# Both MLP up-projections computed with the tokens, not the weights, as the stationary operand

## The chip, the cores and the metric

The kernel runs on one core of one Trainium2 chip. The metric is the device time of one execution in microseconds (us), the median of several runs. TensorE (PE in the rows; PEld is its weight load) multiplies, VectorE (DVE) and ScalarE (ACT) work elementwise, GpSimd (POOL) sets a few constants and issues a few transfers, and SyncE (SP) issues the large ones.

## The reference

Two transformer-like blocks over 256 tokens of width 2048: a gated linear attention block with an MLP, then a block of three branches (windowed attention, a linear recurrence, a short convolution) with an MLP. All inputs are float32. The change concerns the two MLPs alone, which have this form, with 2048 inputs, 8192 hidden columns and 2048 outputs:

```python
def _sq_relu_mlp(h, w_up, w_down):
    a = jax.nn.relu(h @ w_up)
    return (a * a) @ w_down
...
x = x + jnp.square(jax.nn.relu(h @ w_mlp_up[l])) @ w_mlp_down[l]
```

The scale of the normalisation in front of an MLP is applied after its down-projection, since relu and square let a positive factor through.

## The kernel before

**Jobs, chunks and halves.** Every large product is a job: 512 columns of a weight matrix (`KB`) against 128-row pieces of the contraction, called k-tiles; 16 of them in an up-projection job, 32 in a down-projection job. The weights come in chunks of four k-tiles (1 MB, `raw`, three buffers). A half is two k-tiles, and an up-projection job has 8 halves, a down-projection job 16. The 32 up-projection jobs (two MLPs, two groups `hf` of 4096 hidden columns, eight jobs `jn` in each group) have 256 halves. A group's eight up-projection jobs are followed by its four down-projection jobs, so the hidden values of one group live at a time.

**Three products for one.** Each float32 operand is split into a high part that TensorE takes exactly (fp32r) and the remainder. For the weights `split_half` does this for each half: ACT copies 128x1024 elements into `wh` (L186), DVE subtracts to get `wl` (L187). `wh` and `wl` have four buffers each, and `run` splits up to three halves (`LOOK`) ahead of the half that TensorE multiplies. The activations are split in the same way into tiles of [128, 2, 2, 256]: two k-tiles, high and low part, 256 tokens. `x` high times `w` high, `x` high times `w` low and `x` low times `w` high are summed in PSUM.

**Two forms of a job.** In a plain job (`products`) 128 tokens of an activation tile are the stationary operand and 512 weight columns stream past. For each k-tile and each of two groups `t` of 128 tokens there are three matmuls of 512 columns, so a half has 12 matmuls and 6144 columns; the result, [tokens, 512 columns], lies in two PSUM banks. In a swapped job (`swapped`) 128 columns of the weights are stationary and the activations stream: for each k-tile and each of four column groups `n` there is one matmul of 512 columns (`wh` against the high and the low part together, `long`) and one of 256 (`wl` against the high part, `short`). A half has 16 matmuls and 6144 columns, and the result, [columns, tokens], lies in four banks. PSUM has six banks for `acc`. Before the change the up-projections are swapped jobs, since the down-projection wants the hidden values with the hidden columns on the partitions, and a swapped job delivers them so.

**What follows a job.** A job's `ev` is a generator. `tick`, called once after each half, advances one of the waiting generators by a step (two where five or more wait), behind that half's splits in each engine's queue. After an up-projection job `ev` (L637) adds the two halves of each bank with `g_sum` (ACT copies, L330; DVE adds, L331), squares the positive part (L643), and splits into `h` tiles (L647, L651). A down-projection asks for the `h` tiles of up-projection job `jn` at its half 2 x `jn`.

**Turning.** `g_turn` exists before the change, for four stages in which token-order values are split for a later product (for instance after the jobs on `w_out`, L1018, called out2 below, whose jobs are plain and have 8 halves). DVE transposes 32x32 blocks of two 128x512 tiles into `blk` (L294, one buffer). Then 16 copies of 32 partitions move the blocks to their places in `turned`, in four steps of two DVE copies (L305) and two ACT copies (L303). Then come the splits, one pair of k-tiles in a step.

Of the kernel before, what the change touches and what calls it, by code (L numbers as in the profile page):

```python
# [8 lines left out]
F32 = mybir.dt.float32  # L9
F32R = mybir.dt.float32r  # L10
AF = mybir.ActivationFunctionType
ALU = mybir.AluOpType
# [26 lines left out]
def two_blocks(tc, A, out):  # L39
    nc = tc.nc  # L40
    es = ExitStack()
    with es:
# [10 lines left out]
        V, ACT, PE, POOL = nc.vector, nc.scalar, nc.tensor, nc.gpsimd  # L53

        def slot(shape, dt=F32, name="s"):
            return slp.tile(shape, dt, name=name, tag="s")

        def t2(name="t2", shape=(128, 512)):
            return t2p.tile(list(shape), F32, name=name, tag="t2")

        def t1(name="t1"):
            return t1p.tile([128, 256], F32, name=name, tag="t1")
# [7 lines left out]
        def flat(ap):  # L70
            return ap.rearrange("p a b -> p (a b)")
# [36 lines left out]
        def drain(key):  # L108
            rec = gens[key]
            while not rec[2]:  # L110
                if isinstance(rec[1], tuple):
                    drain(rec[1])
                advance(rec)
# [5 lines left out]
        cols = cp.tile([128, 164], F32, name="cols")  # L119
# [143 lines left out]
        def act_tile(name):  # L263
            return slot([128, 2, 2, 256], F32R, name)
# [19 lines left out]
        def split_any(d, src, pr, cols, mul):  # L284
            if cols is None:
                split_pair(d, src, mul)
            else:
                split_cols(d, src, cols[2 * pr:2 * pr + 2])

        def g_turn(full, name, b, cols, mul):  # L290

            blk = t2p.tile([128, 2, 4, 4, 32], F32, name="blk", tag="blk", bufs=1)
            for t in range(2):
                V.transpose(blk[:, t].rearrange("p f q c -> p (f q c)"), full(t))  # L294
            turned = slot([128, 4, 256], F32, "turned")
            to = turned.rearrange("p f (t q c) -> p f t q c", t=2, q=4)
            fr = blk.rearrange("p t f q c -> p f t q c")
            for a in range(4):
                yield 0
                for z in range(4):  # L300
                    o, i = to[32 * z:32 * z + 32, :, :, a, :], fr[32 * a:32 * a + 32, :, :, z, :]
                    if z % 2:
                        ACT.activation(o, i, AF.Copy)  # L303
                    else:
                        V.tensor_copy(o, i)  # L305
            for pr in range(2):
                yield 0
                d = T[name, 2 * b + pr] = act_tile("a")
                split_any(d, turned[:, 2 * pr:2 * pr + 2, :], pr, cols, mul)

        def g_split(full, name, b, cols=None, mul=None):
            if b < 3:
                yield from g_turn(full, name, b, cols, mul)
                return

            def src(t, i):
                return full(t)[:, i * 128:(i + 1) * 128]
            tps = [pair_transpose(src, 0)]
            yield 0
            tps.append(pair_transpose(src, 1))  # L320
            for pr in range(2):
                d = T[name, 2 * b + pr] = act_tile("a")
                split_any(d, tps[pr], pr, cols, mul)
                if pr == 0:
                    yield 0

        def g_sum(acc, dst):
            for n in range(4):
                r = t1("right")
                ACT.activation(r, acc[n][:, 256:512], AF.Copy)  # L330
                V.tensor_tensor(dst[:, n, :], acc[n][:, 0:256], r, op=ALU.add)  # L331
# [31 lines left out]
        def xblk(t, b):  # L363
            return xres[:, t, b * KB:(b + 1) * KB]
# [11 lines left out]
        T = {}  # L376
# [32 lines left out]
        def acts(name):  # L409
            return lambda k: T[name, k // 2][:, k % 2]  # L410
# [205 lines left out]
        def job(w, c0, nk, act, ev, key, need=None, pre=None, swap=False):  # L616
            jobs.append(Job(w[:, c0:c0 + KB], list(range(nk)), act, ev, key, need, pre, swap))
# [16 lines left out]
        def mlp(tag, w_up, w_down, xname, xkeys, rskey, rsq, ev_last):  # L634
            for hf in range(2):
                for jn in range(8):
                    def ev(acc, hf=hf, jn=jn):  # L637
                        y = slot([128, 4, 256], F32, "up")
                        g_sum(acc, y)
                        yield 0  # L640
                        for p in range(2):
                            v = flat(y[:, 2 * p:2 * p + 2, :])
                            V.scalar_tensor_tensor(v, v, 0.0, v, op0=ALU.max, op1=ALU.mult)  # L643
                        yield 0
                        for p in range(2):
                            d = T[tag, hf, 2 * jn + p] = act_tile("h")
                            ACT.activation(d[:, :, 0, :], y[:, 2 * p:2 * p + 2, :], AF.Copy)  # L647
                        yield 0
                        for p in range(2):
                            d = T[tag, hf, 2 * jn + p]  # L650
                            V.tensor_tensor(d[:, :, 1, :], y[:, 2 * p:2 * p + 2, :], d[:, :, 0, :].bitcast(F32), op=ALU.subtract)  # L651
                    job(w_up, hf * 4096 + jn * KB, 16, acts(xname), ev, (tag + "up", hf, jn),
                        (lambda k: ((xkeys, k // 4),)) if hf == 0 and jn == 0 else None, swap=True)
                for n in range(4):
                    def lhs(k, hf=hf):
                        return T[tag, hf, k // 2][:, k % 2]
                    if hf == 0:
                        def ev(acc, n=n):
                            drain(rskey)
                            for t in range(2):  # L660
                                V.scalar_tensor_tensor(xblk(t, n), acc[t], rsq[:, t:t + 1], xblk(t, n), op0=ALU.mult, op1=ALU.add)
                            yield 0
                    else:
                        ev = ev_last(n)
                    job(w_down[hf * 4096:(hf + 1) * 4096, :], n * KB, 32, lhs, ev, (tag + "dn", hf, n),
                        (lambda k, hf=hf: ((tag + "up", hf, k // 4),)) if n == 0 else None,
                        pre=pre_dn.get((tag, hf, n)))
# [30 lines left out]
        def ev_last1(n):  # L698
# [10 lines left out]
            return f  # L709

        mlp("m1", A["mlp_w_up"][0], A["mlp_w_down"][0], "x2", "out1", "rs2", T["rs2q"], ev_last1)


# [322 lines left out]
        def ev_last2(n):  # L1036
# [28 lines left out]
            return final if n == 3 else f  # L1065

        mlp("m2", A["w_mlp_up_2"][0], A["w_mlp_down_2"][0], "x5", "out2", "rs5", T["rs5q"], ev_last2)


# [81 lines left out]
```

## Time and profile before

| | us |
|---|---|
| median of 3 runs (2684.74 to 2685.83) | 2685.81 |
| profiled execution, device time | 2687.48 |
| its span, first to last instruction | 2685.7 |
| TensorE busy in the span | 2664.9 |
| VectorE busy | 1656.4 |
| ScalarE busy | 1315.5 |
| mean transfer rate | 191 GB/s |

The span of the profiled execution leaves out 1.78 us of its device time. A matmul's record lasts longer than the distance to the next one, since matmuls are pipelined: the pace is read from how many start in a stretch, not from a record's duration. Mean granted TensorE clock over the span is 0.998 of the full 2.4 GHz.

### The profile page before, as it was taken

The numbers are of one execution on the slowest core, as the hardware profiler recorded it, in microseconds if no ns is written. First come the engines' busy times: TensorE is split into PE (matmuls) and PEld (weight loads), VectorE is DVE, ScalarE is ACT, GpSimd is POOL, SyncE is SP. The second block draws the span as 40 slices with busy tenths as digits, with TensorE's granted clock in tenths as the row PEclk, the third lists the DMA queues.
The fourth block names the chain that finished last, engine by engine and source line by source line (L and its number), as shares of the span: only waits on it lengthen the run. The fifth ranks groups of instructions, "written<-read, shape, count | busy, mean of one in ns | idle before, by whom it ended". The sixth has DMA issues, their size and how long they took to land.

```text
span 2685.7 us, 32831 instructions
## 1 busy us (share of the span) xinstructions
PE 2664.9 (99%) x13234; PEld 2251.7 (84%) x13234; DVE 1656.4 (62%) x2105; ACT 1315.5 (49%) x1703; POOL 20.0 (1%) x44
## 2 busy tenths in 40 slices
PE   9999999999999999999999999999999999999998
PEld 7886788888888888888888888888888888888887
DVE  5575776664456665667887556566666654466554
ACT  5554665453344455544555444445554443444443
POOL 0000000000000000000000000000000000000000
PEclk9999999999999999999999999999999999999999
DMA  7553555555555655665556555565555555556554
GB/s 254 190 187 127 167 186 187 189 194 191 191 193 191 206 191 189 203 221 188 183 191 229 190 173 180 194 203 198 188 188 188 189 195 196 188 188 204 194 197 141
DMA packets 258105, 513.20 MB, mean 191 GB/s; under 512 B 10472, under 2 KB 12656, under 8 KB 257824
## 3 DMA queue, kind: packets, MB, share of 16 engines
q1 hardware_dynamic: 255232, 501.51, 56.9%
q0 software_dynamic: 2576, 9.50, 1.1%
q8 instruction: 103, 1.69, 0.3%
q14 instruction: 50, 0.41, 0.0%
q10 hardware_dynamic: 144, 0.08, 0.0%
HBM read 508.96 MB, written 3.68 MB: 191 GB/s over the span
## 4 chain that ended last, share of the span: by engine, by line
PE 98%; DVE 1%; DMA 0%; ACT 0%; SPq 0%; issue 0%; DVEq 0%; ACTq 0%
PE acc L194 96%; DMA raw<-in_gla_w_in 0%; PE po L194 0%; PE sc L194 0%; PE gate L194 0%; PE as L194 0%; PE ao L194 0%; DVE wl L187 0%; PE tp L260 0%; PE z L194 0%; SPq L397 0%; DVE oh L584 0%; PE tg L194 0%; DVE turned L305 0%; SPq L163 0%
## 5 line engine op out<-in xcount | busy, mean ns | idle before, releaser
L187 DVE TENSOR_TENSOR wl<-raw,wh 128x1024 fp32r<-128x1024 f32 x942 | 1151.8, 1224 | 924.7 <-ACT wh L186 923.9
L186 ACT ACTIVATE wh<-raw 128x1024 fp32r<-128x1024 f32 x942 | 997.4, 1059 | 1170.0 <-PE acc L194 1112.7
L194 PE MATMUL acc<-a,wh 128*128 128x512 f32 x3200 | 797.0, 393 | 5.1 <-DVE a L282 3.4
L194 PEld LDWEIGHTS acc<-a,wh 128*128 128x128 f32 x3200 | 578.4, 189 | 108.6 <-DVE a L282 4.1
L194 PE MATMUL acc<-wh,h 128*128 128x512 f32 x2048 | 631.4, 389 | 0.0
L194 PE MATMUL acc<-wh,a 128*128 128x512 f32 x1920 | 610.9, 394 | 3.5 <-ACT a L281 3.2
L194 PEld LDWEIGHTS acc<-a,wl 128*128 128x128 f32 x3200 | 431.0, 190 | 29.9 <-issue 0.6
L194 PEld LDWEIGHTS acc<-wh,h 128*128 128x128 f32 x2048 | 384.4, 188 | 79.8
L194 PE MATMUL acc<-a,wl 128*128 128x256 f32 x3200 | 440.3, 282 | 0.0
L194 PEld LDWEIGHTS acc<-wh,a 128*128 128x128 f32 x1920 | 360.8, 188 | 85.9 <-issue 5.7
L194 PE MATMUL acc<-wl,h 128*128 128x512 f32 x1024 | 398.3, 389 | 0.0
L194 PE MATMUL acc<-wl,a 128*128 128x512 f32 x960 | 374.5, 390 | 0.0
L194 PEld LDWEIGHTS acc<-wl,h 128*128 128x128 f32 x1024 | 192.2, 188 | 39.9
L194 PEld LDWEIGHTS acc<-wl,a 128*128 128x128 f32 x960 | 180.6, 188 | 37.9 <-issue 1.4
L330 ACT ACTIVATE right<-acc 128x256 f32<-128x256 f32 x200 | 77.0, 385 | 78.0 <-PE acc L194 67.1
L331 DVE TENSOR_TENSOR up<-acc,right 128x256 f32<-128x256 f32 x128 | 54.4, 425 | 18.5 <-ACT right L330 15.3
L303 ACT ACTIVATE turned<-blk 32x256 f32<-32x256 f32 x120 | 49.8, 415 | 6.5 <-DVE blk L294 4.4
L643 DVE SCALAR_TENSOR_TENSOR up<-up 128x512 f32<-128x512 f32 x64 | 41.2, 686 | 0.0
L651 DVE TENSOR_TENSOR h<-up,h 128x512 fp32r<-128x512 f32 x64 | 41.1, 684 | 0.0
L194 PE MATMUL acc<-wh,yl 128*128 128x512 f32 x128 | 40.9, 393 | 0.0
L194 PE MATMUL acc<-wh,yc 128*128 128x512 f32 x128 | 40.7, 393 | 0.0
L194 PE MATMUL acc<-wh,ya 128*128 128x512 f32 x128 | 40.1, 389 | 0.0
(253 smaller groups left out, 961.0 us busy)
## 6 DMA issues: line engine op xcount, KB each, us to landing
raw<-in_w_in SPq DMA_DIRECT2D x112, 1024.0 KB, 5.2
raw<-in_mlp_w_up SPq DMA_DIRECT2D x64, 1024.0 KB, 5.2
raw<-in_mlp_w_down SPq DMA_DIRECT2D x64, 1024.0 KB, 5.1
raw<-in_w_mlp_up SPq DMA_DIRECT2D x64, 1024.0 KB, 5.1
raw<-in_w_mlp_down SPq DMA_DIRECT2D x64, 1024.0 KB, 5.1
raw<-in_gla_w_in SPq DMA_DIRECT2D x46, 1024.0 KB, 5.1
raw<-in_gla_w_out SPq DMA_DIRECT2D x16, 1024.0 KB, 5.1
raw<-in_w_out SPq DMA_DIRECT2D x16, 1024.0 KB, 5.1
```

Of the source, the lines that this page charges most:

```text
L186: ACT.activation(flat(wh), flat(src), AF.Copy)
L187: V.tensor_tensor(flat(wl), flat(src), flat(wh.bitcast(F32)), op=ALU.subtract)
L194: PE.matmul(o, l, r, start=a, stop=b)
L303: ACT.activation(o, i, AF.Copy)
L330: ACT.activation(r, acc[n][:, 256:512], AF.Copy)
L331: V.tensor_tensor(dst[:, n, :], acc[n][:, 0:256], r, op=ALU.add)
L643: V.scalar_tensor_tensor(v, v, 0.0, v, op0=ALU.max, op1=ALU.mult)
L651: V.tensor_tensor(d[:, :, 1, :], y[:, 2 * p:2 * p + 2, :], d[:, :, 0, :].bitcast(F32), op=ALU.subtract)
```

## The change

`mlp` makes its up-projections plain jobs. Relu and square are now done on the two PSUM banks in token order, one 128x512 ACT and one 128x512 DVE instruction for each bank, into `t2` tiles; then `g_turn` brings the result to column order, and its last step splits both pairs of k-tiles at once (`rest=0`). The down-projections read the tiles under a new key and are otherwise as they were.

```diff
-        def g_turn(full, name, b, cols, mul):
+        def g_turn(full, name, b, cols, mul, rest=1):
...
             for pr in range(2):
-                yield 0
+                if rest or not pr:
+                    yield 0
                 d = T[name, 2 * b + pr] = act_tile("a")
                 split_any(d, turned[:, 2 * pr:2 * pr + 2, :], pr, cols, mul)
...
                     def ev(acc, hf=hf, jn=jn):
-                        y = slot([128, 4, 256], F32, "up")
-                        g_sum(acc, y)
+                        ys = []
+                        for t in range(2):
+                            y = t2("up")
+                            ACT.activation(y, acc[t], AF.Relu)
+                            V.tensor_tensor(y, y, acc[t], op=ALU.mult)
+                            ys.append(y)
                         yield 0
-                        for p in range(2):
-                            v = flat(y[:, 2 * p:2 * p + 2, :])
-                            V.scalar_tensor_tensor(v, v, 0.0, v, op0=ALU.max, op1=ALU.mult)
-                        yield 0
-                        for p in range(2):
-                            d = T[tag, hf, 2 * jn + p] = act_tile("h")
-                            ACT.activation(d[:, :, 0, :], y[:, 2 * p:2 * p + 2, :], AF.Copy)
-                        yield 0
-                        for p in range(2):
-                            d = T[tag, hf, 2 * jn + p]
-                            V.tensor_tensor(d[:, :, 1, :], y[:, 2 * p:2 * p + 2, :], d[:, :, 0, :].bitcast(F32), op=ALU.subtract)
+                        yield from g_turn(lambda t: ys[t], (tag, hf), jn, None, None, 0)
                     job(w_up, hf * 4096 + jn * KB, 16, acts(xname), ev, (tag + "up", hf, jn),
-                        (lambda k: ((xkeys, k // 4),)) if hf == 0 and jn == 0 else None, swap=True)
+                        (lambda k: ((xkeys, k // 4),)) if hf == 0 and jn == 0 else None)
                 for n in range(4):
                     def lhs(k, hf=hf):
-                        return T[tag, hf, k // 2][:, k % 2]
+                        return T[(tag, hf), k // 2][:, k % 2]
```

On TensorE, the first half of an up-projection job (the third of the first group) stands like this before; in a row's name the first operand behind the arrow streams and the second is stationary, and `acc` is a PSUM bank.

```order
L194 MATMUL acc_3450<-a_2851,wh_3375 128x512 x2
L194 MATMUL acc_3450<-a_2851,wl_3376 128x256 x2
L194 MATMUL acc_3451<-a_2851,wh_3375 128x512 x2
L194 MATMUL acc_3451<-a_2851,wl_3376 128x256 x2
L194 MATMUL acc_3452<-a_2851,wh_3375 128x512 x2
L194 MATMUL acc_3452<-a_2851,wl_3376 128x256 x2
L194 MATMUL acc_3453<-a_2851,wh_3375 128x512 x2
L194 MATMUL acc_3453<-a_2851,wl_3376 128x256 x2
```

The first k-tile of the same job on TensorE now, which is the first half of a half:

```order
L194 MATMUL acc_3409<-wh_3353,a_2851 128x512
L194 MATMUL acc_3409<-wl_3354,a_2851 128x512
L194 MATMUL acc_3409<-wh_3353,a_2851 128x512
L194 MATMUL acc_3410<-wh_3353,a_2851 128x512
L194 MATMUL acc_3410<-wl_3354,a_2851 128x512
L194 MATMUL acc_3410<-wh_3353,a_2851 128x512
```

Sixteen matmuls in four banks have become twelve in two, all of 512 columns.

On VectorE, what follows the second up-projection job of that group before, among the weight splits (L187) of the next one:

```order
L331 TENSOR_TENSOR up_3437<-acc_3227,right_3438 128x256
L331 TENSOR_TENSOR up_3437<-acc_3228,right_3441 128x256
L331 TENSOR_TENSOR up_3437<-acc_3229,right_3444 128x256
L331 TENSOR_TENSOR up_3437<-acc_3230,right_3447 128x256
L187 TENSOR_TENSOR wl_3455<-raw_3286,wh_3454 128x1024
L643 SCALAR_TENSOR_TENSOR up_3437<-up_3437 128x512 x2
L187 TENSOR_TENSOR wl_3479<-raw_3343,wh_3478 128x1024
L187 TENSOR_TENSOR wl_3503<-raw_3343,wh_3502 128x1024
L651 TENSOR_TENSOR h_3498<-up_3437,h_3498 128x2x256
L651 TENSOR_TENSOR h_3500<-up_3437,h_3500 128x2x256
```

What follows the third job on VectorE now:

```order
L643 TENSOR_TENSOR up_3573<-up_3573,acc_3409 128x512
L643 TENSOR_TENSOR up_3576<-up_3576,acc_3410 128x512
L187 TENSOR_TENSOR wl_3582<-raw_3457,wh_3581 128x1024
L294 STREAM_TRANSPOSE blk_3599<-up_3573 128x512
L294 STREAM_TRANSPOSE blk_3599<-up_3576 128x512
L187 TENSOR_TENSOR wl_3604<-raw_3499,wh_3603 128x1024
L305 COPY turned_3602<-blk_3599 32x8x32 x2
L187 TENSOR_TENSOR wl_3624<-raw_3499,wh_3623 128x1024
L305 COPY turned_3602<-blk_3599 32x8x32 x2
L187 TENSOR_TENSOR wl_3646<-raw_3543,wh_3645 128x1024
```

Two more such copy steps follow, each behind a weight split, and one split later the two subtractions of the activation split (L270). The step with the squares is followed by six others, one behind each weight split, so that the work spreads over seven halves where it took four.

## Rows read from the trace of the kernel before

**Rows 1.** The page: busy us and share of TensorE; the chain that ended last.
```profile
PE 2664.9 (99%) x13234; PEld 2251.7 (84%) x13234; DVE 1656.4 (62%) x2105; ACT 1315.5 (49%) x1703; POOL 20.0 (1%) x44
PE 98%; DVE 1%; DMA 0%; ACT 0%; SPq 0%; issue 0%; DVEq 0%; ACTq 0%
```

**Rows 2.** Whom TensorE waited for: total us, times, longest; the two longest.
```profile
PE acc L194 <- DVE a L282: 3.8, 3, 2.3
PE acc L194 <- ACT a L281: 3.2, 2, 2.6
```

**Rows 3.** Stretches: up-projection groups, one down-projection group, one out2 job (last).
```profile
core 0: us, PE busy (x) PEld busy (x) DVE busy (x) ACT busy (x) POOL busy (x), PEclk, DMA share, GB/s
407.96:586.98 179.02, 179.02 (x1033) 157.99 (x1032) 111.30 (x138) 90.33 (x119) 0.00 (x0) 1.00 0.59 189
...
761.06:939.20 178.14, 178.14 (x1026) 157.18 (x1025) 107.79 (x124) 86.16 (x109) 1.73 (x3) 1.00 0.61 195
939.20:1113.28 174.08, 174.08 (x770) 144.14 (x769) 104.66 (x126) 91.26 (x128) 0.51 (x1) 1.00 0.59 193
...
2324.41:2502.55 178.14, 178.14 (x1026) 157.18 (x1025) 107.80 (x124) 86.17 (x109) 1.07 (x2) 1.00 0.61 196
...
1905.10:1926.90 21.80, 21.80 (x98) 18.04 (x97) 15.35 (x23) 14.40 (x24) 0.00 (x0) 1.00 0.58 194
```

**Rows 4.** The chain of waits in order: start us, us, what, matmuls.
```profile
413.69 0.44 PE tp L260 x4
...
1135.17 153.09 PE acc L194 x880
...
1703.92 184.99 PE acc L194 x816
```

**Rows 5.** One up-projection job, 784.0 to 805.8: busy us, mean ns, idle before.
```profile
L187 DVE TENSOR_TENSOR wl<-raw,wh 128x1024 fp32r<-128x1024 f32 x8 | 9.8, 1224 | 8.0 <-ACT wh L186 8.0
...
L186 ACT ACTIVATE wh<-raw 128x1024 fp32r<-128x1024 f32 x8 | 8.5, 1059 | 9.8 <-PE acc L194 9.8
...
L331 DVE TENSOR_TENSOR up<-acc,right 128x256 f32<-128x256 f32 x4 | 1.7, 424 | 0.6 <-ACT right L330 0.5
L330 ACT ACTIVATE right<-acc 128x256 f32<-128x256 f32 x4 | 1.5, 385 | 1.5 <-PE acc L194 1.3
L643 DVE SCALAR_TENSOR_TENSOR up<-up 128x512 f32<-128x512 f32 x2 | 1.3, 686 | 0.0
L651 DVE TENSOR_TENSOR h<-up,h 128x512 fp32r<-128x512 f32 x2 | 1.3, 682 | 0.0
L647 ACT ACTIVATE h<-up 128x512 fp32r<-128x512 f32 x2 | 1.1, 618 | 0.0
```

**Rows 6.** Groups of the whole run: forms nearest to the added instructions.
```profile
L294 DVE STREAM_TRANSPOSE blk<-xres 128x512 f32<-128x512 f32 x18 | 11.7, 687 | 0.0
...
L583 ACT ACTIVATE th<-acc,rs1h 128x512 f32<-128x512 f32 x8 | 5.2, 685 | 1.0 <-PE acc L194 0.9
...
L609 DVE TENSOR_TENSOR xres<-acc,xres 128x512 f32<-128x512 f32 x8 | 5.1, 683 | 0.0
...
L568 ACT ACTIVATE junk<-po 128x512 f32<-128x512 f32 x8 | 4.8, 599 | 23.0 <-PE po L194 23.0
```

**Rows 7.** The out2 job of rows 3, 1905.1 to 1926.9: the turn's copies.
```profile
L303 ACT ACTIVATE turned<-blk 32x256 f32<-32x256 f32 x8 | 3.3, 415 | 0.1
L305 DVE COPY turned<-blk 32x256 f32<-32x256 f32 x8 | 2.3, 284 | 0.1
```

**Rows 8.** Waits of the weight splits, 762 to 1113: total us, times, longest.
```profile
ACT wh L186 <- PE acc L194: 151.5, 108, 2.7
DVE wl L187 <- ACT wh L186: 134.3, 110, 2.5
```

**Rows 9.** TensorE in order of time where it waited for turned values.
```profile
320.11 0.50 PE L194 MATMUL acc<-wh,a 128*128 128x512 f32 x1 [0.63 <-ACT a L281]
...
329.02 0.50 PE L194 MATMUL acc<-wh,a 128*128 128x512 f32 x1 [2.57 <-ACT a L281]
```

## The prediction

> **What bounds the kernel now.** I read the page first, for the share of busy time and the chain that ended last: TensorE is busy for 2664.9 of 2685.7 us, and 98% of the chain is TensorE [rows 1]. That does not yet say that it works at its best pace, so I read next whom it waited for. The two longest totals are 3.8 and 3.2 us in the whole span [rows 2], and both belong to values that come out of a turn (L281, L282) early in the run, where a first job asks for them at once [rows 9]. In the MLPs there is no such wait. So the bound in the stage that the change touches is the number and pace of TensorE's matmuls, and the third view is the one that counts: stretches that begin and end at the first matmul of a group. An up-projection group and a down-projection group have the same number of halves, 64, of the same 6144 columns, and both run at a granted clock of 1.00, the 2.4 GHz level. The up-projections take 178.14 us, the down-projections 174.08 us [rows 3]. The first group of each MLP takes 179.02 us; the extra 0.88 us are two groups of four transposes of 0.44 us each that stand between its matmuls [rows 4] and stay there.
>
> **What the change takes from TensorE.** The chain of waits has two long unbroken pieces, one of swapped jobs alone and one of plain jobs alone [rows 4]. Swapped: 153.09 us for 880 matmuls, and 16 make a half: 153.09 / 880 x 16 = 2.7835 us. Plain: 184.99 / 816 x 12 = 2.7204 us. The difference is 0.063 us a half, and 256 halves change their form: 16.2 us. The stretches give the same by another way: 178.14 - 174.08 = 4.06 us a group, and four groups give 16.2 us. Where it comes from: at 2.4 GHz the 6144 columns of a half need 2.56 us, so the swapped half carries 0.224 us beyond its columns and the plain one 0.160 us. A plain matmul carries 0.2267 - 0.2133 = 0.0134 us; four matmuls fewer explain 0.054 of the 0.063 us. The plain pace is not an estimate from another data shape: down-projections and the piece of 816 matmuls have different stationary tiles and agree to 0.001 us a half.
>
> Here a rule can be set against the rows. The rows show about 13 ns for each matmul beyond its columns [rows 4]. The Trainium skill, "TensorE: Matmul & The Clock Gate", section "Back-to-back issue gap", gives the isolated warm gap as N / 2.4 + 2.5 ns, which is an estimate of 2.600 us for a swapped half and 2.590 us for a plain one, so 10 ns a half and 2.6 us in all: 2683.2 us. By that rule the change would be lost in the measurement; the trace does not agree with it (226.7 ns where it says 215.8), and I take the trace.
>
> **What the change puts on the other engines.** Per up-projection job, before, DVE has 8 weight splits of 1.224 us, 4 additions of 0.424, 2 squares of 0.686 and 2 subtractions of 0.682: 9.79 + 1.70 + 1.37 + 1.36 = 14.2 us. ACT has 8 x 1.059 + 4 x 0.385 + 2 x 0.618 = 11.2 us [rows 5]. After it, DVE has the same 9.79 us of splits, 2 products out of PSUM (nearest row L609, 0.683), 2 transposes of 0.687, 8 copies of 0.284 and 2 subtractions of 0.682: 9.79 + 1.37 + 1.37 + 2.27 + 1.36 = 16.2 us. ACT has 8.47 us of splits, 2 relus out of PSUM (bounds 0.599 and 0.685 from the nearest rows, a square without and a tanh with a scale operand; I take 0.6, since relu has no scale operand here), 8 copies of 0.415 and 2 splits of 0.618: 8.47 + 1.2 + 3.32 + 1.24 = 14.2 us [rows 5 to 7]. A plain job lasts 8 x 2.72 = 21.8 us. DVE goes from 14.2 to 16.2 us of it, ACT from 11.2 to 14.2; neither fills it, and no relu brings a table load with it in the changed order. These 2 and 3 us cost nothing as long as the weight splits stay ahead.
>
> That cover is the lead of three halves. ACT waits for TensorE to free a buffer 108 times in the 351 us of two groups, for 151.5 us, and DVE waits for ACT [rows 8]; TensorE waits for neither. Take the worst place, the end of a job at time zero. Behind the two relus (1.2 us) the next ACT split is queued (1.06), behind that the DVE split (1.22): ready at about 3.5 to 3.7 us with the gaps between instructions. TensorE needs it three halves later, at 8.2 us, so 4.5 us are left. The relus hold two PSUM banks, and the next job uses two of the four others, so it does not wait for them. Every later step is within one half: the heaviest on DVE is a split with two transposes or with two subtractions, 1.22 + 1.37 = 2.6 us, the heaviest on ACT a split with two activation splits or relus, 1.06 + 1.24 = 2.3 us, under 2.72 us both. So no lag builds up.
>
> The best evidence is a stage that already does this. An out2 job is plain, has 8 halves, a turn with the same copies [rows 7], and more besides (squares with sums, scaled splits). A stretch of 21.8 us in it holds 97 to 98 matmuls (a job has 96), DVE busy for 15.35 and ACT for 14.40 us [rows 3]: about the load I expect of the changed jobs, and TensorE keeps its plain pace and waits for nothing there.
>
> The down-projection asks for the tiles of the last up-projection job at its half 14. In the changed order they are split seven halves after the job's end, so seven halves, 19 us, are left. The chunks of weights now go by in 174.1 us a group instead of 178.1; the down-projection groups draw them at that pace already, 193 GB/s [rows 3]. SP's queue keeps its transfers in the same order, and POOL has nothing to do here but transfers whose users come a whole job later.
>
> **The sum.** Span 2685.7 - 16.2 = 2669.5 us; with the 1.78 us that lie around the span of the profiled execution 2671.3 us. The median of the runs lies 1.67 us below that execution, so the forecast for the median is 2685.81 - 16.2 = 2669.6 us.
>
> **The rivals.** First, partial loss: TensorE runs at the plain pace but waits briefly at the job ends, where relus and products stand ahead of a split. A quarter of a microsecond at each of 32 ends gives 8 us back: 2677.7 us. For it speaks that 2 to 3 us are added to each job's queues, against it the 4.5 us of lead.
>
> Second, no gain: the excess of a half does not belong to the form but to the place (these x tiles, these weights), or goes with columns. Then the plain half costs 2.78 us here too and the time stays at 2685.8 us. If the cost beyond the columns went with the half and not with the matmul, both forms would carry the same; the rows give 0.224 and 0.160 us, and 16 to 12 is nearly the ratio of these two. Plain jobs with different operands speak against it as well [rows 3, 4]. Its mild form: only a sixth of the 13 ns goes with the matmul and the rest with the columns; then a sixth of the gain is left, 16.2 / 6 = 2.7 us, and the time is 2683.1 us. The page's rule above is of this form.
>
> Third, slower, by one mechanism: the lockstep of ACT and DVE. DVE stands idle for 8.0 us in an up-projection job, waiting for ACT's splits [rows 5]. If that idle time were a cost of the handshake that stays, and not room left over because ACT itself waits for TensorE, a job would need 16.2 + 8.0 = 24.2 us on DVE against 21.8 on TensorE. That is 2.4 us more for each of 32 jobs: 2669.6 + 78 = 2747 us. It decides from 22.3 us a job on, where the 16.2 us of gain are eaten up (16.2 / 32 = 0.5 us a job). Against it: ACT's own idle time before these splits, 9.8 us, ends with TensorE [rows 5], and in the out2 job DVE does as much within 21.8 us. TensorE does wait for turns in this kernel, 0.63 and 2.57 us at a time [rows 9], but there a job asks for them within six halves of the job that makes them, not after fourteen.
>
> **How the numbers follow.** The forecast, 2669.6 us, has a chance of 0.87, partial loss 0.06, no gain 0.03 (0.01 of it for its mild form), slower 0.04. Fast and slow by more than 0.2% (5.4 us, about what a measurement of this kernel can tell from no change) mean below 2680.4 and above 2691.2 us. Partial loss is mostly still faster: faster 0.92, same 0.04, slower 0.04. The range takes the forecast with what is uncertain in it: the runs before differ by 1.1 us, the relu's bounds touch nothing on the path, and the gain by its two ways differs by 0.1 us. A little lost lead at some job ends is likelier than a gain beyond the plain pace, so the range reaches 2.6 us down and 5.4 us up: 2667 to 2675 us.
>
> **What would show it.** Right: all four up-projection groups within 0.5 us of 174.1 us (175.0 with the transposes), 768 matmuls of 512 columns in each, TensorE's list of waits without L187, L186 or the turn's lines in the MLPs, DVE at about 16.2 and ACT at about 14.2 us a job. Partial loss: new waits of TensorE for `wl` or `wh` at intervals of 21.8 us. No gain: 178 us a group without waits. Slower: groups of 190 us or more, TensorE waiting for `wl` in every job. I am wrong if the turn's copies are slower beside plain up-projections than in out2, or if the lead of three halves is not there when relus take its place.

## The result and the profile after

| | us |
|---|---|
| before, median of 6 runs (2684.74 to 2687.59) | 2685.81 |
| changed kernel, median of 6 runs (2668.26 to 2670.71) | 2669.72 |
| ratio, with its 95% interval | 0.9939 [0.9927, 0.9952] |
| profiled execution after, device time | 2668.26 |
| its span | 2666.5 |

The change takes 16.1 us off. The page of the changed kernel, busy time and chain, answers to [rows 1]:

```profile
PE 2646.8 (99%) x12210; PEld 2198.2 (82%) x12210; DVE 1716.4 (64%) x2297; ACT 1411.7 (53%) x1895; POOL 20.0 (1%) x44
PE 98%; DVE 1%; DMA 0%; ACT 0%; SPq 0%; issue 0%; DVEq 0%; ACTq 0%
```

TensorE has 1024 matmuls fewer (32 jobs x 8 halves x 4), DVE 60 us and ACT 96 us more to do, and the chain is still TensorE's. The stretches of the changed kernel, in the order of the program: an up-projection group, a down-projection group and the second up-projection group of the first MLP, then both up-projection groups of the second (columns as in [rows 3]):

```profile
404.82:579.86 175.04, 175.04 (x778) 144.93 (x776) 123.96 (x178) 110.86 (x159) 0.00 (x0) 1.00 0.60 192
579.86:753.94 174.08, 174.08 (x770) 144.15 (x769) 88.47 (x85) 72.89 (x76) 0.00 (x0) 1.00 0.57 193
753.94:928.02 174.08, 174.08 (x770) 144.14 (x769) 120.50 (x164) 106.64 (x149) 1.74 (x3) 1.00 0.62 200
1960.13:2135.17 175.04, 175.04 (x778) 144.93 (x776) 124.09 (x178) 110.83 (x159) 0.00 (x0) 1.00 0.60 193
2309.25:2483.33 174.08, 174.08 (x770) 144.14 (x768) 120.49 (x164) 106.61 (x149) 1.07 (x2) 1.00 0.62 200
```

All four up-projection groups now last what a down-projection group lasts, the first of each MLP with the transposes on top. The fourth group of before, whose row [rows 3] leave out, was the first of the second MLP:

```profile
1971.31:2150.33 179.02, 179.02 (x1033) 157.99 (x1032) 111.40 (x138) 90.31 (x119) 0.00 (x0) 1.00 0.59 189
```

The sum over the four was 179.02 + 178.14 + 179.02 + 178.14 = 714.32 us and is 175.04 + 174.08 + 175.04 + 174.08 = 698.24 us: 16.1 us less, the whole difference of the medians. One changed job in the second group, one job's length by line, answers to [rows 5]:

```profile
L187 DVE TENSOR_TENSOR wl<-raw,wh 128x1024 fp32r<-128x1024 f32 x8 | 9.8, 1221 | 5.6 <-ACT wh L186 5.6
L186 ACT ACTIVATE wh<-raw 128x1024 fp32r<-128x1024 f32 x8 | 8.5, 1060 | 6.4 <-PE acc L194 5.6 <-ACT turned L303 0.8
...
L303 ACT ACTIVATE turned<-blk 32x256 f32<-32x256 f32 x8 | 3.3, 417 | 0.4 <-DVE blk L294 0.3
L305 DVE COPY turned<-blk 32x256 f32<-32x256 f32 x8 | 2.3, 283 | 0.1
L643 DVE TENSOR_TENSOR up<-up,acc 128x512 f32<-128x512 f32 x3 | 2.1, 688 | 0.7 <-ACT up L642 0.7
L642 ACT ACTIVATE up<-acc 128x512 f32<-128x512 f32 x3 | 1.8, 598 | 1.1 <-PE acc L194 1.0
L294 DVE STREAM_TRANSPOSE blk<-up 128x512 f32<-128x512 f32 x2 | 1.3, 688 | 0.0
L270 DVE TENSOR_TENSOR a<-turned,a 128x512 fp32r<-128x512 f32 x2 | 1.3, 682 | 0.0
L269 ACT ACTIVATE a<-turned 128x512 fp32r<-128x512 f32 x2 | 1.1, 614 | 0.0
```

The stretch catches a third relu and product at its edge; a job has two of each. DVE's idle time ahead of its splits fell from 8.0 us [rows 5] to 5.6: it was room, and the turn took it. ACT still waits for TensorE ahead of its splits. The two longest of the waits of TensorE in the changed kernel, which answer to [rows 2]:

```profile
PE acc L194 <- ACT a L281: 3.2, 2, 2.6
PE acc L194 <- DVE a L282: 2.4, 3, 1.2
```

No wait of TensorE belongs to the MLPs. The span of the profiled execution fell by 19.2 us, 3.1 more than the groups gave. Those 3.1 us lie ahead of the first MLP, in code that did not change, and are no part of the effect; the last section tells what differs there.

### The profile page after: what moved, and what is told of

Its sections match the earlier page's. It is cut to its first block, busy times and chain, and to the rows that moved or that the text cites. A ratio compares the mean times of both kernels' runs of the same rounds, so it can differ in the third digit from the quotient of the medians.

```text
span 2666.5 us, 31193 instructions
## 1 busy us (share of the span) xinstructions
PE 2646.8 (99%) x12210; PEld 2198.2 (82%) x12210; DVE 1716.4 (64%) x2297; ACT 1411.7 (53%) x1895; POOL 20.0 (1%) x44
## 4 chain that ended last, share of the span: by engine, by line
PE 98%; DVE 1%; DMA 0%; ACT 0%; SPq 0%; issue 0%; DVEq 0%; ACTq 0%
PE acc L194 96%; DMA raw<-in_gla_w_in 0%; PE po L194 0%; PE sc L194 0%; PE gate L194 0%; PE as L194 0%; PE ao L194 0%; DVE wl L187 0%; PE tp L260 0%; PE z L194 0%; SPq L398 0%; DVE oh L585 0%; PE tg L194 0%; DVE turned L305 0%; SPq L163 0%
## 5 line engine op out<-in xcount | busy, mean ns | idle before, releaser
L194 PE MATMUL acc<-wh,a 128*128 128x512 f32 x6016 | 1871.7, 390 | 3.5 <-ACT a L281 3.2
L187 DVE TENSOR_TENSOR wl<-raw,wh 128x1024 fp32r<-128x1024 f32 x942 | 1150.3, 1222 | 848.3 <-ACT wh L186 847.6
L194 PEld LDWEIGHTS acc<-wh,a 128*128 128x128 f32 x6016 | 1129.0, 188 | 245.2 <-issue 5.7
L194 PE MATMUL acc<-wl,a 128*128 128x512 f32 x3008 | 1170.6, 389 | 0.0
L194 PEld LDWEIGHTS acc<-wl,a 128*128 128x128 f32 x3008 | 564.7, 188 | 117.6 <-issue 1.4
L194 PE MATMUL acc<-a,wh 128*128 128x512 f32 x1152 | 289.3, 394 | 3.9 <-DVE a L282 2.1
L194 PEld LDWEIGHTS acc<-a,wh 128*128 128x128 f32 x1152 | 208.0, 189 | 42.0 <-DVE a L282 2.8
L303 ACT ACTIVATE turned<-blk 32x256 f32<-32x256 f32 x376 | 156.6, 416 | 18.9 <-DVE blk L294 13.1
L194 PEld LDWEIGHTS acc<-a,wl 128*128 128x128 f32 x1152 | 156.4, 191 | 11.4 <-issue 0.6
L194 PE MATMUL acc<-a,wl 128*128 128x256 f32 x1152 | 160.6, 284 | 0.0
L305 DVE COPY turned<-blk 32x256 f32<-32x256 f32 x376 | 106.4, 283 | 6.9
L270 DVE TENSOR_TENSOR a<-turned,a 128x512 fp32r<-128x512 f32 x64 | 41.1, 684 | 0.0
```

The costliest lines, as they stand in the source:

```text
L187: V.tensor_tensor(flat(wl), flat(src), flat(wh.bitcast(F32)), op=ALU.subtract)
L194: PE.matmul(o, l, r, start=a, stop=b)
L270: V.tensor_tensor(l, src, h.bitcast(F32), op=ALU.subtract)
```

## Experiments

**The theory** is that of the prediction: the gain is 0.063 us for each half that goes from 16 matmuls to 12, TensorE alone sets the time, and DVE and ACT have room as long as weight splits keep their lead. The rivals: a gain with another cause (once, not per half; or bound to columns), and a cost on DVE and ACT that has been paid or hidden by luck. A time without an interval is that of a single run; there the stretches of its profile carry the reading.

**Half the change.** The first MLP changed, the second as before.

```diff
-                        (lambda k: ((xkeys, k // 4),)) if hf == 0 and jn == 0 else None)
+                        (lambda k: ((xkeys, k // 4),)) if hf == 0 and jn == 0 else None, swap=tag == "m2")
...
+                        if tag == "m2":
+                            y = slot([128, 4, 256], F32, "up")
+                            g_sum(acc, y)
...
+                            return
```

> The change in the first MLP alone; the second keeps swapped up-projections and the old steps behind them. My theory: half of the gain, 128 halves x 0.063 = 8.1 us, 2677.7 us; the two groups of the first MLP last 175.0 and 174.1 us, those of the second 179.0 and 178.1 us. Rival (the gain is no sum over halves but a stall that the old form caused once, or at one place): nearly all of the gain or none, 2670 or 2686 us.

Measured: 2676.67 us against 2686.02, ratio 0.9968 [0.9957, 0.9980]. The second group of the first and of the second MLP:

```profile
754.45:928.53 174.08, 174.08 (x769) 144.15 (x768) 120.50 (x164) 106.62 (x149) 1.73 (x3) 1.00 0.61 200
2313.75:2491.88 178.13, 178.13 (x1025) 157.17 (x1024) 107.79 (x124) 86.12 (x109) 1.07 (x2) 1.00 0.61 196
```

Each group has the time of its form, to 0.01 us. The gain is a sum over halves, and the groups do not touch each other. The median fell by 9.35 us where 8.1 were forecast; the groups give the 8.1, and the rest is no more than the stretch ahead of the first MLP varies (last section).

**The same columns in more matmuls.** All but the first and the last product of each bank are cut in two.

```diff
-                        mm(acc[t], xh, wl[:, i], False, False)
+                        for c in cuts:
+                            mm(acc[t][:, c], xh, wl[:, i, c], False, False)
```

> In the up-projection jobs 92 of 96 matmuls are cut into two of 256 columns (the first and the last product of each bank stay whole): the same columns, 92 more matmuls in a job. My theory (about 13 ns for each matmul beyond its columns; 0.120 us for 256 columns against 0.2267 for 512): 92 x (2 x 0.120 - 0.2267) = 1.2 us a job, 39 us in all, groups of 183.9 us, 2709 us. Rival (the excess goes with the half or with its columns): 2669.7 us. The mild form, 2.5 ns for a matmul: 92 x 32 x 0.0025 = 7.4 us, 2677 us.

Measured: 2708.99 us. The second up-projection group of the first MLP:

```profile
765.13:949.08 183.95, 183.95 (x1505) 182.51 (x1504) 120.83 (x164) 106.55 (x149) 1.73 (x3) 1.00 0.63 190
```

183.95 us where 183.9 were forecast: the excess does not go with the columns or the half, and the mild form of that rival (2677 us) is ruled out with it. One reservation: the weight loads fill 182.51 of the 183.95 us here, so that 0.120 us for 256 columns may be the columns and 13 ns, or the load of 128 stationary columns that stands behind each. Both give this number. The fill alone does not decide it, since each load's record lasts 0.191 us and overlaps the next one's.

**Half the stationary columns.** The same 92 of 96 matmuls with 64 tokens in place of 128.

```diff
-                        mm(acc[t], xh, wl[:, i], False, False)
+                        mm(acc[t][0:n1, :], xh[:, 0:n1], wl[:, i], False, False)
```

> In the up-projection jobs the same 92 of 96 matmuls use only the first 64 of 128 tokens as the stationary operand, so half of the hidden values lack most of their sums. Number and columns of the matmuls are unchanged. If the 13 ns beyond the columns belong to the matmul itself: no change, groups of 174.1 us, 2669.7 us. If they belong to the loading of the stationary columns: half of them go, 92 x 32 x 0.0067 = 20 us, groups of 169.2 us, 2650 us.

Measured: 2679.86 us, a miss for both expectations: the jobs became slower.

```profile
758.01:934.60 176.59, 176.59 (x769) 104.75 (x768) 120.57 (x164) 106.59 (x149) 1.74 (x3) 1.00 0.61 197
```

The loads did become shorter, 104.75 / 768 = 0.136 us each where [rows 3] give 144.14 / 769 = 0.187, and yet the distance of the matmuls rose by 2.5 / 768 = 0.003 us. So at 512 columns the 13 ns do not shrink with the number of stationary columns. Why a smaller stationary tile costs 3 ns was not found.

**The turn on TensorE.** Eight transposes of 128x128 a job in place of the DVE blocks and the copies.

```diff
-                        yield from g_turn(lambda t: ys[t], (tag, hf), jn, None, None, 0)
+                        for pr in range(2):
+                            tp = pair_transpose(lambda t, i: ys[t][:, i * 128:(i + 1) * 128], pr)
+                            yield 0
+                            d = T[(tag, hf), 2 * jn + pr] = act_tile("a")
+                            split_pair(d, tp)
+                            yield 0
```

> Plain up-projections, but the turn is made by TensorE transposes (eight 128x128 in a job, 0.44 us for four) in place of DVE blocks and 16 copies; DVE and ACT have about 4 and 3 us less to do in each job. My theory (TensorE's own time alone counts): 0.88 us more for each of 32 jobs, 28 us on top of 2669.7: 2698 us, slower than the kernel before by 12 us. Rival (the load on DVE and ACT matters for TensorE's pace): less than 28 us are added, since that load falls.

Measured: 2700.62 us against 2686.02, ratio 1.0056 [1.0042, 1.0070]. The second up-projection group and the down-projection group behind it:

```profile
763.82:944.62 180.80, 180.80 (x825) 149.65 (x824) 97.56 (x94) 82.77 (x93) 0.00 (x0) 1.00 0.58 187
944.62:1119.66 175.04, 175.04 (x777) 144.97 (x776) 103.83 (x123) 91.41 (x128) 0.51 (x1) 1.00 0.57 193
```

(180.80 - 174.08 + 175.04 - 174.08) / 8 = 0.96 us a job, a little over the 0.88 forecast, though DVE has some 23 us less to do in the group. What frees DVE and ACT buys nothing, and what is put on TensorE is paid in full: with this turn the change would have lost 14.6 us.

**More load on DVE and ACT.** The copies of the turn behind an up-projection, made n = 2 and n = 4 times.

```diff
+                    for _ in range(n if mul is None and cols is None else 1):
```

> Each of the 16 copies of the turn behind an up-projection is made twice: DVE 16.2 + 2.3 = 18.5 us and ACT 14.2 + 3.3 = 17.5 us of a job's 21.8 us. My theory (room until an engine fills 21.8 us, lead of three halves): no change, groups of 174.1 us, 2669.7 us. Rival of the prediction (lockstep: DVE's 8 us of waiting stay): 18.5 + 8 = 26.5 us a job, over 2800 us. Partial: waits of TensorE at the job ends, up to 0.5 us each, 2686 us.

> Each of the 16 copies of the turn behind an up-projection is made four times: ACT 8.5 + 1.2 + 4 x 3.3 + 1.2 = 24.2 us and DVE 9.8 + 1.4 + 1.4 + 4 x 2.3 + 1.4 = 23.0 us a job, both over 21.8 us. My theory: ACT becomes the bound of the up-projection groups, 24.2 us a job, groups of about 194 us, 2748 us, with TensorE waiting for wl or wh. Rival (the lead of three halves swallows it): 2669.7 us.

Measured: twice 2670.34 us, four times 2820.91 us. The second up-projection group of either:

```profile
755.97:930.04 174.07, 174.07 (x769) 144.16 (x768) 135.80 (x220) 129.06 (x205) 1.74 (x3) 1.00 0.62 199
```

```profile
793.71:999.16 205.45, 184.64 (x769) 142.47 (x767) 160.73 (x328) 169.22 (x313) 1.74 (x3) 1.00 0.51 165
```

Twice the copies cost nothing; at that load the lockstep rival is out. With four times the direction was right and the size was not: 205.45 us where about 194 were forecast, and ACT is busy for only 169 of them. The order of time on ACT in the group's second job, the first with such a turn behind it:

```profile
819.72 3.53 ACT L304 ACTIVATE turned<-blk 32x256 f32<-32x256 f32 x8 [0.27 <-DVE blk L294]
...
824.36 3.53 ACT L304 ACTIVATE turned<-blk 32x256 f32<-32x256 f32 x8
```

In each of the four halves with copies ACT needs 824.36 - 819.72 = 4.64 us against TensorE's 2.72, a weight split between the copies included: it falls 4 x 1.92 = 7.7 us behind. The lead hides most of that once. The second job and the fourth, as stretches:

```profile
815.47:838.28 22.81, 22.23 (x98) 17.76 (x96) 17.62 (x42) 20.30 (x41) 0.00 (x0) 1.00 0.45 148
865.10:891.90 26.80, 23.43 (x97) 17.78 (x97) 22.03 (x47) 23.31 (x45) 0.00 (x0) 1.00 0.49 158
```

From the third job on the lead is used up, each job lasts 26.8 us, and ACT never waits for a buffer of TensorE. It waits for DVE, and DVE waits for ACT. In the stretch of the fourth job, ACT ahead of the copies, DVE at the same time, and DVE's idle time ahead of its splits:

```profile
868.84 2.00 ACT L186 ACTIVATE wh<-raw 128x1024 fp32r<-128x1024 f32 x2
873.35 3.53 ACT L304 ACTIVATE turned<-blk 32x256 f32<-32x256 f32 x8 [2.51 <-DVE blk L294]
```

```profile
869.70 1.27 DVE L644 TENSOR_TENSOR up<-up,acc 128x512 f32<-128x512 f32 x2
...
872.03 1.29 DVE L294 STREAM_TRANSPOSE blk<-up 128x512 f32<-128x512 f32 x2
```

```profile
L187 DVE TENSOR_TENSOR wl<-raw,wh 128x1024 fp32r<-128x1024 f32 x9 | 10.9, 1216 | 4.6 <-ACT wh L186 4.6
```

ACT's 23.3 us of work, 2.5 us of waiting for DVE's transposes and some 1.0 us of gaps between its instructions make the 26.8 us. DVE in its turn stood idle for 4.6 us of the job until ACT's splits came, and so reaches the transposes late. So past the room the two engines do hold each other up, which is the lockstep rival in a form that the prediction did not have. The loss is (205.45 + 180.35 - 2 x 174.08) / 8 = 4.7 us a job, the down-projection group behind (180.35 us, with the last job's turn) counted in, where the sum of ACT's work alone gave 2.4. A job's sum of busy time tells whether there is room, and not what it costs to be past it.

**The lead itself.** Weight splits one half ahead in place of three, in the changed kernel and in the one before.

```diff
-                look = min(LOOK, 1 + s // 3)
+                look = min(1 if s < len(halves) - 4 else LOOK, 1 + s // 3)
```

> The changed kernel with weight splits put into the queues one half ahead in place of three (the buffers stay). My theory: at each job end the split of the next half but one stands behind the relus and is ready 3.5 to 3.7 us after the job's last matmul, while TensorE wants it 2.72 us after: about 0.9 us lost at each of the 32 ends, groups of 181 us; other stages lose as well. Rival (the turn's copies in the middle of a job are the tight place, not the ends): waits spread over the halves, groups over 185 us.

> The kernel before with weight splits put into the queues one half ahead in place of three (the buffers stay). At a job end four ACT copies of 0.385 us stand ahead of the split, where the changed kernel has two relus of 0.6 us: ready about 4.2 us after the job's last matmul, wanted after 2.78 us. My theory: about 1.4 us lost at each end, up-projection groups of about 189 us, so the old form leans on the lead at least as much as the new one. Rival (the swapped form is more patient): groups under 181 us.

Measured: 2716.03 and 2729.46 us. The second up-projection group of the changed kernel with that lead, and of the one before:

```profile
768.59:944.60 176.01, 176.01 (x770) 143.62 (x768) 118.74 (x164) 103.08 (x147) 1.73 (x3) 1.00 0.60 197
```

```profile
772.59:951.95 179.36, 179.36 (x1026) 157.70 (x1025) 105.99 (x124) 82.24 (x107) 1.73 (x3) 1.00 0.59 194
```

The loss at a job end is (176.01 - 174.08) / 8 = 0.24 us, not 0.9, and (179.36 - 178.14) / 8 = 0.15 us, not 1.4. Both forecasts were too high, and the second one's rival came true: the old form's group stays under 181 us and loses less there than the new one's. So the old form does not lean on the lead more than the new one in these groups. Most of what these runs lost lies outside the MLPs: the stretch between the two MLPs went from 858.0 to 880.9 us in the first and to 881.0 in the second. In the changed kernel the place is the one forecast, as the order of time at a job end of the changed kernel with the short lead shows:

```profile
789.87 1.28 ACT L642 ACTIVATE up<-acc 128x512 f32<-128x512 f32 x2 [6.42 <-PE acc L194]
...
790.50 1.37 DVE L643 TENSOR_TENSOR up<-up,acc 128x512 f32<-128x512 f32 x2 [5.79 <-ACT up L642]
...
791.04 2.00 ACT L186 ACTIVATE wh<-raw 128x1024 fp32r<-128x1024 f32 x2
...
792.13 1.23 DVE L187 TENSOR_TENSOR wl<-raw,wh 128x1024 fp32r<-128x1024 f32 x1 [0.26 <-ACT wh L186]
...
793.41 0.19 PEld L194 LDWEIGHTS acc<-wl,a 128*128 128x128 f32 x1 [0.37 <-DVE wl L187]
```

TensorE's next half begins near 790.4, 2.72 us ahead of the half that waits here, in the weight load of its second matmul. The first relu starts half a microsecond earlier than that, since the bank of the first 128 tokens is complete three matmuls before the job's end. The split is ready at 793.36, 3.0 us after the half's beginning, and not at 3.5 to 3.7.

**More jobs in the plain form.** The 14 swapped jobs of the second block's input projection, turned straight out of PSUM; then the same turn spread over four steps; then three jobs of the first block as well. The changed kernel ran again beside the last two.

```diff
+        def turn_into(acc, dst):
+            blk = t2p.tile([128, 2, 4, 4, 32], F32, name="blk", tag="blk", bufs=1)
+            for t in range(2):
+                V.transpose(blk[:, t].rearrange("p f q c -> p (f q c)"), acc[t])
...
-                g_sum(acc, xs)
+                turn_into(acc, xs)
...
-            job(w2, 3072 + b * KB, 16, X3, ev_xr(b), ("xr", b), swap=True)
+            job(w2, 3072 + b * KB, 16, X3, ev_xr(b), ("xr", b))
```

In steps, `turn_into` yields behind every fourth copy, `tick` puts a started turn first, and the callers use `yield from`.

> The same exchange on 14 more jobs: the swapped jobs of the second block's input projection become plain, and their result is turned straight out of PSUM in one go (2 transposes, 10 DVE and 6 ACT copies), with the job's scaling as before. My theory (0.063 us for each half that changes form, covered by the lead of three halves): 14 x 8 x 0.063 = 7.1 us off the changed kernel, 2662.6 us. Rival (the gain belongs to the MLPs, or the busier DVE and ACT queues of this stage with its scans and reciprocals eat it): 2669.7 us or more, with waits of TensorE for weight splits between about 1102 and 1580 us.

> e9 with its turn out of PSUM spread over four steps (four copies behind each weight split, a started turn goes ahead of other steps) in place of one go; nothing else differs. My theory: what e9 lost of its 7.1 us were late weight splits at a few job ends, behind 16 copies queued at once and the stage's own DVE work; with the copies spread these waits go, and the stretch between the two MLPs lasts 851.0 us (858.03 in the changed kernel, 854.8 in e9), about 2662.7 us. Rival (the stage's scans, reciprocals and scalings alone fill the queues): the waits stay, 854 to 855 us.

> e10 and the same exchange for the three swapped jobs of the first block that are not the run's first job. My theory: 3 x 8 x 0.063 = 1.5 us less again, in the stretch ahead of the first MLP, about 2661.2 us. Rival (the later arrival of the turned q and k delays the attention heads, for which TensorE waits): no gain or a loss in that stretch.

> The changed kernel once more, beside e10 and e11 on the same chip: 2669.7 us by its six runs; the four up-projection groups at 175.0 and 174.1 us as in its first profile, and the stretch ahead of the first MLP anywhere between 404.8 and 408.0 us, since that stretch varied so between kernels that are the same in it.

| | median us | ratio to before, interval | between the MLPs, us |
|---|---|---|---|
| e9_more_plain | 2666.73 | 0.9929 [0.9917, 0.9942] | 854.79 |
| e10_turn_in_steps | 2671.81 | 0.9944 [0.9932, 0.9957] | 859.52 |
| e11_all_but_first | 2668.24 | 0.9931 [0.9919, 0.9943] | 859.5 |
| after_again | 2669.94 | 0.9936 [0.9922, 0.9949] | 858.03 |

The first version gains 3.2 us of 7.1 in its stretch. The other 3.9 us went to late splits, for which TensorE's matmuls wait three times and its weight loads six times in that version:

```profile
PE acc L194 <- DVE wl L187: 1.8, 3, 0.7
PEld acc L194 <- DVE wl L187: 4.1, 6, 1.1
```

Four of the six, 2.9 us of the 4.1, stand behind a turn made in one go, as my account had it. DVE ahead of the first of them, in that version:

```profile
1194.49 1.23 DVE L187 TENSOR_TENSOR wl<-raw,wh 128x1024 fp32r<-128x1024 f32 x1 [0.51 <-ACT wh L186]
...
1196.98 2.98 DVE L340 COPY col<-blk 32x256 f32<-32x256 f32 x10
...
1201.18 1.22 DVE L187 TENSOR_TENSOR wl<-raw,wh 128x1024 fp32r<-128x1024 f32 x1
```

Spreading the copies did away with these four: up to 1371 us the second version (e10_turn_in_steps) has no wait for a split in that stretch. But the stretch as a whole became longer, 859.52 us, slower than in the changed kernel, since new and longer waits came behind it. So my account of the waits was half right, and the forecast of 851.0 us wrong. The loads' waits in the second version, and the longest one:

```profile
PEld acc L196 <- DVE wl L189: 7.6, 7, 3.1
```

```profile
1374.54 0.29 PEld L196 LDWEIGHTS acc<-wl,a 128*128 128x128 f32 x1 [3.14 <-DVE wl L189]
```

DVE ahead of it does this:

```profile
1362.11 1.23 DVE L189 TENSOR_TENSOR wl<-raw,wh 128x1024 fp32r<-128x1024 f32 x1 [2.81 <-ACT wh L188]
...
1367.29 1.22 DVE L189 TENSOR_TENSOR wl<-raw,wh 128x1024 fp32r<-128x1024 f32 x1
...
1370.15 1.20 DVE L813 TENSOR_TENSOR xs<-xs,R 128x1024 f32<-128x1024 f32 x1
...
1371.84 1.52 DVE L820 SCALAR_TENSOR_TENSOR xc<-xs,cols,xc 128x255 f32<-128x255 f32 x3
1373.27 1.22 DVE L189 TENSOR_TENSOR wl<-raw,wh 128x1024 fp32r<-128x1024 f32 x1
```

Three splits follow each other at 5 to 6 us where TensorE uses one in 2.72. Between them stands this stage's own work, the scan and the convolution of two generators, not the copies. Each extra step keeps generators alive longer, and where five wait, `tick` lets two of them put work ahead of the next split. The last reason is read from the code and the order; no run separates it. TensorE's clock adds to it. Behind the longest wait, 2.7 us for the matmul, it was granted in part:

```profile
1371.00:1381.00 10.00, 6.91 (x24) 4.99 (x23) 9.61 (x20) 2.11 (x2) 0.00 (x0) 0.83 0.25 83
```

The three jobs of the first block gave nothing that can be told from the variation of their stretch; the median with them is 3.6 us lower where 1.5 were forecast, and the intervals overlap. The first version is thus the shortest time seen, though its interval overlaps that of the changed kernel; its gain is sure in the stretch (854.79 against 858.03 us, which the changed kernel repeated to 0.01 us).

## Why the prediction was right

**TensorE's pace: right.** 16.2 us were forecast, 16.1 measured, in the groups named and to 0.1 us each. Cutting the matmuls gave the forecast 39 us, so the number of matmuls, each with its weight load, and not columns, is what the swapped form paid for. The split of the 0.063 us into 0.054 for four matmuls and a rest was not tested, nor whether the 256-column pace is set by its load. That the medians too agree to 0.1 us is in part luck: the stretch ahead of the first MLP varies by 3 us from one profile to another, and the median of the half change fell by 1.3 us more than its groups did.

**The rule of the Trainium skill: out.** The trace of the changed kernel has 174.08 us / 768 = 0.2267 us a matmul, 13 ns over its columns, as before. By the isolated gap that the Trainium skill gives ("TensorE: Matmul & The Clock Gate", section "Back-to-back issue gap"), N / 2.4 + 2.5 ns, the change would have ended near 2683 us, an estimate from that formula; the trace does not agree with it.

**The load on DVE and ACT: right.** 16.2 and 14.2 us a job were forecast; the rows give 9.8 + 1.4 + 1.3 + 2.3 + 1.3 = 16.1 and 8.5 + 1.2 + 3.3 + 1.1 = 14.1 us, with the relu at 0.598 us on its lower bound. That it is free was shown by doubling the copies at no cost.

**The lead: right in kind, the size off.** A split at a job end is ready 3.0 us after the next half's beginning, not 3.5 to 3.7; some 8.2 - 3.0 = 5.2 us of lead are left and not 4.5. The step forgot that the first of the two banks is complete before the job's end. It erred on the safe side and did not touch the forecast.

**The rivals.** No partial loss is seen: no wait in the MLPs, and the groups are at the plain pace to the last 0.01 us. The lockstep fell with the doubled copies and with DVE's idle time, which shrank. With four times the copies, where the sum of 24.2 us is past a job's 21.8 as well, it came back: 2.5 us of ACT's waiting for DVE a job, and a loss of twice what the sum says.

**A reading that was wrong.** Of the 3.8 us that TensorE waits for L282 [rows 2], only 0.3 belong to a turn. The other 3.4 us stand in the run's first job, before 24 us, where DVE splits the input (`xt`). Neither place is in the MLPs, so the forecast did not hang on it. Two sums among the rivals are rounded loosely: 32 x 2.4 us is 77 and not 78, and 2669.6 + 8 is 2677.6; nothing hangs on them.

## What to carry to other kernels

Where TensorE sets the time, count its matmuls and not only their columns: the same product in fewer and longer matmuls is worth the difference of their measured distances, and a turn that this costs may go to engines that wait. A job's busy sum tells whether there is such room: at 18.5 of 21.8 us the added work was free, with the splits three halves ahead. Past it the sum is too low a price, since engines that feed each other then wait for each other too. Of a stage that already carries several generators, the same exchange gave half of what it promised.

## What the runs showed of the hardware

Fewer stationary columns made matmuls of 512 columns slower, by 3 ns each, while their loads became shorter by a quarter.

After the same idle time of 2.57 us [rows 9] TensorE's clock was granted in part in some executions and in full in others. The stretch of 9 us that holds this wait, before and in the changed kernel:

```profile
325.00:334.00 9.00, 6.43 (x24) 4.69 (x23) 6.19 (x14) 6.24 (x14) 0.00 (x0) 0.81 0.36 126
```

```profile
323.45:332.45 9.00, 6.43 (x30) 4.87 (x29) 6.93 (x15) 7.26 (x15) 0.00 (x0) 1.00 0.35 117
```

The first has a mean of 0.81 of the 2.4 GHz level, so part of it ran at 1.2, and six matmuls fewer. In eleven profiles the program is the same up to there and the wait 2.56 to 2.57 us; six of them show the 0.81 and five the 1.00, and the fall costs 1.5 to 1.6 us. This and a start that differed by 1.5 us are the 3.1 us by which the two profiled spans differ beyond the groups; across the kernels of the study, apart from the two with the short lead, that stretch ended between 404.8 and 408.0 us. A profile of one execution can thus mislead by 3 us here, more than the forecast's error, and the stretches by group are the better measure.
